# Strassen products in the first MLP of a two-layer decoder step, with the residual stream kept in DRAM

## The chip, the cores and the metric

The kernel runs on one core of one Trainium2 chip, in one launch. The metric is the device time of the launch in microseconds (us), the median of several executions. One more execution was taken with a hardware profile; its rows are the ones read below. A core has one matmul engine (TensorE, PE in the rows, its weight loads PEld), a vector engine (VectorE, DVE), a scalar engine (ScalarE, ACT), GpSimd (POOL), and queues that issue DMA transfers (SP's, ACT's and POOL's among them). Each engine takes its instructions strictly in the order in which they stand in its own list; a matmul result goes into PSUM banks and is read from there by DVE or ACT.

## The reference, cut to what matters

One step of a decoder with two layers runs on 512 prompt tokens and 8 sample tokens; the kernel treats them as one block of 520 columns. Layer 0 mixes tokens by causal pooling and then runs an MLP; after it, keys and values are projected once (`w_kv`), and layer 1 attends over them, projects, and runs its own MLP. What the change touches is the MLP:

```
def _rmsnorm(x, g):
    return x * lax.rsqrt(jnp.mean(x * x, axis=-1, keepdims=True) + RMS_EPS) * g

def _mlp_block(x, g, w_up, w_down):
    h = jnp.square(jax.nn.relu(_rmsnorm(x, g) @ w_up))   # 1024 -> 4096
    return x + h @ w_down                                # 4096 -> 1024
```

The samples also need 'summaries' of their cached pages (`_compress`: blocks of 32 cached rows times `cmp_w1`, then SiLU, then `cmp_w2`). They depend on the cache alone, so the kernel makes them beside the first MLP.

## The kernel before, in words

**Layout.** x stands transposed in SBUF, `xT`, as 8 tiles of 128 features by 520 tokens. Every large matmul is 128x128 weights against 260 columns, in a 32-bit format that keeps fewer mantissa bits. For full precision each operand is split in a rounded part and the rest (`whi`/`wlo`, `xh`/`xl`, `hh`/`hl`), and three products are summed: hi by hi, hi by rest, rest by hi. ACT rounds (L147, L181), DVE subtracts (L148, L182).

**Normalisation is deferred.** Since the MLP squares a ReLU, the kernel multiplies the unnormalised x by the gain alone, and scales the result by 1/mean(x^2) (`rstd2`) behind the down projection. The mean needs the squares of all 8 tiles: ACT squares, POOL adds six of them into `sqacc` (`add_square`, L224), PE sums over the partitions (`mean_tok`, L235), DVE reads the sums (L240, L242). `spread` (L245) makes the 128x520 `rstd2` from them: diagonal tiles on DVE (L250), two matmuls (L252, L253).

**Layer 0's MLP before** (`mlp`, L615) is the plain product. `split_x` (L260) makes xh and xl of each of the 8 tiles of x as soon as it is ready. `dense` (L151) makes 48 matmuls for each of 32 tiles of 128 hidden features, and as many for each of the 8 output tiles in each of 4 chunks of the down projection: 32x48 + 32x48 = 3072. It works in four PSUM banks under the tag `mm`. `yacc` (128x8x520) collects the output. Between tiles the loop takes a step of a filler, `compress_samples`, which gathers pages by POOL's indirect DMA (L361), permutes them (L372), transposes them on PE (L385), splits them (ACT L386, DVE L387) and multiplies them (L391) into two PSUM banks that stay taken until it ends. Those two are of the four banks under the tag `aux`.

**Layer 1's MLP before** (`fast_mlp`, L690) multiplies in quarters by Strassen's rule, in Winograd's form: for 256 hidden features the product of 2x2 blocks of weights with 2x2 blocks of x takes 7 products (`product`, L185) of 12 matmuls, 84 in place of 96. For that, `fast_w` (L313) makes three sums of weight blocks on DVE, and `fast_x` (L273) makes seven left-hand terms of x: for each j of 0 to 3 it scales tiles j and j+4 on ACT (L281), makes four sums and differences on DVE (L291, L292, L294, L297) and splits seven terms (ACT L286, DVE L287). The three terms `first` have tiles of their own, the four others take the place of xh and xl. The down projection is plain, in 8 chunks of 512 hidden features, 16 products of 12 matmuls in each, into the `aux` banks; its products stand between those of the next chunk's up projection.

**Order.** A scheduler sets each engine's list from the code's order and its own estimates; what it made of the start of the first MLP is shown below for both kernels.

## Time and profile before

| | us |
|---|---|
| median of 3 timed runs | 1197.63 (1195.52 to 1200.01) |
| the profiled execution | 1202.7 |
| its span in the trace | 1200.9 |
| PE busy in the span | 1156.1 (96%) |

Within the span the first MLP goes from about 50 us (the end of the pooling mixer's projection) to 452 us, keys and values follow, then attention, the output projection until 829 us, and layer 1's MLP from there to the end. The profile gives for each engine its busy time, the clock that the throttle granted TensorE in each stretch (1.00 is the level of 2.4 GHz, 0.5 that of 1.2 GHz), and for each wait what ended it. A row of a timeline is: start, duration, engine, line, operation, the tile written and the tiles read, and in square brackets the idle time ahead of it with what released it. Where instructions overlap in the engine's pipeline, the distance between two starts is the price of one, not the duration.

### The profile page before, as it was taken

Reading aid. Unit: us, or ns where it says so; the run is one execution under the profiler, and the core shown is the slowest. Engines: PE = TensorE matmul, PEld = TensorE weight load, DVE = VectorE, ACT = ScalarE, POOL = GpSimd, SP = SyncE. Lnnn points to the kernel's source line nnn. Section 1 sums busy time; section 2 is a strip of 40 time slices with the busy share of each in tenths; the row PEclk is TensorE's granted clock in tenths of the full one; section 3 lists DMA queues with packets and bytes.
Section 4 is the critical chain, followed back from the end, with each engine's and each line's share of the span. In section 5 each row is a group of like instructions: output and inputs, shape, how many; then the busy total and the mean of one; then the engine's idle time right before and its main releaser. Section 6 shows DMA issues by size and latency. Waiting matters only on the chain.

```text
span 1200.9 us, 22704 instructions
## 1 busy us (share of the span) xinstructions
PE 1156.1 (96%) x9163; PEld 1081.8 (90%) x9163; DVE 747.5 (62%) x1732; ACT 544.0 (45%) x1152; POOL 253.6 (21%) x287
## 2 busy tenths in 40 slices
PE   4999999999999999999899999979999999999996
PEld 4999999999999999999876566778999999999996
DVE  5844234444453574576588677648966686776885
ACT  4443233223323433453366565725764443544445
POOL 3500000000031020243358544631000000000032
PEclk9899999999999999999999999989999999999998
DMA  9454333324223236443411220261223323333201
GB/s 258 153 192 141 97 98 122 92 86 132 71 72 123 71 106 211 131 106 100 89 36 45 72 71 19 44 178 61 80 97 106 106 71 115 97 106 106 72 35 72
DMA packets 106511, 121.30 MB, mean 101 GB/s; under 512 B 5640, under 2 KB 93312, under 8 KB 106143
## 3 DMA queue, kind: packets, MB, share of 16 engines
q1 hardware_dynamic: 93159, 103.42, 28.0%
q0 software_dynamic: 4224, 12.17, 3.0%
q10 hardware_dynamic: 9024, 4.28, 1.3%
q8 instruction: 72, 1.18, 0.4%
q14 instruction: 32, 0.26, 0.1%
HBM read 111.50 MB, written 12.98 MB: 104 GB/s over the span
## 4 chain that ended last, share of the span: by engine, by line
PE 90%; DVE 4%; DMA 3%; ACT 1%; issue 1%; SPq 0%; DVEq 0%; ACTq 0%
PE mm L160 45%; PE mm L190 14%; PE aux L190 13%; PE mm L1151 3%; PE aux L1198 3%; PE aux L1225 3%; PE aux L391 2%; DMA wraw<-in_pool_w_dram 1%; DMA wraw<-in_w_up_dram 1%; DVE wlo L148 1%; PE aux L1023 1%; DMA spill<-xT 1%; PE aux L435 1%; PE mm L576 1%; PE aux L385 1%
## 5 line engine op out<-in xcount | busy, mean ns | idle before, releaser
L147 ACT ACTIVATE whi<-wraw 128x1024 fp32r<-128x1024 f32 (+1 forms) x95 | 99.9, 1055 | 302.3 <-PE mm L160 291.7
L160 PE MATMUL mm<-xh,whi 128*128 128x260 f32 (+1 forms) x976 | 208.5, 287 | 9.2 <-DVE xT L1298 5.8
L160 PE MATMUL mm<-xl,whi 128*128 128x260 f32 (+1 forms) x976 | 208.3, 287 | 0.8 <-issue 0.6
L160 PE MATMUL mm<-xh,wlo 128*128 128x260 f32 (+1 forms) x976 | 207.1, 286 | 0.4 <-issue 0.4
L148 DVE TENSOR_TENSOR wlo<-wraw,whi 128x1024 fp32r<-128x1024 f32 (+1 forms) x95 | 119.4, 1259 | 131.5 <-ACT whi L147 131.1
L160 PEld LDWEIGHTS mm<-xh,whi 128*128 128x128 f32 (+1 forms) x976 | 155.8, 190 | 11.9 <-DVE xT L1298 6.0
L160 PEld LDWEIGHTS mm<-xl,whi 128*128 128x128 f32 (+1 forms) x976 | 155.4, 190 | 1.9 <-issue 1.1
L160 PEld LDWEIGHTS mm<-xh,wlo 128*128 128x128 f32 (+1 forms) x976 | 155.1, 190 | 1.3 <-issue 1.0
L190 PE MATMUL aux<-hl,whi 128*128 128x260 f32 x448 | 125.2, 282 | 0.0
L190 PE MATMUL aux<-hh,whi 128*128 128x260 f32 x448 | 124.8, 282 | 0.0
L190 PE MATMUL aux<-hh,wlo 128*128 128x260 f32 x448 | 122.6, 283 | 0.0
L181 ACT ACTIVATE whi<-wraw 128x512 fp32r<-128x512 f32 x112 | 66.3, 626 | 106.6 <-PE mm L190 83.0
L160 PE MATMUL mm<-hh,whi 128*128 128x260 f32 x512 | 103.1, 283 | 0.0
L160 PE MATMUL mm<-hh,wlo 128*128 128x260 f32 x512 | 103.0, 283 | 0.0
L160 PE MATMUL mm<-hl,whi 128*128 128x260 f32 x512 | 103.0, 282 | 0.0
L182 DVE TENSOR_TENSOR wlo<-wraw,whi 128x512 fp32r<-128x512 f32 x112 | 75.5, 698 | 30.4 <-ACT whi L181 29.7
L1184 POOL TENSOR_SCALAR s<-s,psm,gate 128x128 f32<-128x128 f32 (+3 forms) x128 | 79.9, 637 | 41.3 <-DVE psm L1181 14.0
L190 PEld LDWEIGHTS aux<-hl,whi 128*128 128x128 f32 x448 | 84.3, 188 | 0.0
L190 PEld LDWEIGHTS aux<-hh,whi 128*128 128x128 f32 x448 | 84.1, 188 | 0.0
L190 PEld LDWEIGHTS aux<-hh,wlo 128*128 128x128 f32 x448 | 82.7, 188 | 0.0
L779 POOL TENSOR_TENSOR yacc<-yacc,xT 128x520 f32<-128x520 f32 x8 | 11.3, 1407 | 330.4 <-DVE yacc L778 327.0
L160 PEld LDWEIGHTS mm<-hh,whi 128*128 128x128 f32 x512 | 79.3, 188 | 0.7
(338 smaller groups left out, 2617.7 us busy)
## 6 DMA issues: line engine op xcount, KB each, us to landing
wraw<-in_w_up_dram SPq DMA_DIRECT2D x32, 1024.0 KB, 6.4
wraw<-in_w_down_dram SPq DMA_DIRECT2D x32, 1024.0 KB, 5.1
wraw<-in_w_kv_dram SPq DMA_DIRECT2D x6, 1024.0 KB, 4.9
w<-in_cmp_w_dram ACTq DMA_DIRECT2D x32, 128.0 KB, 5.0
wraw<-in_w_qg_dram SPq DMA_DIRECT2D x8, 512.0 KB, 8.3
wraw<-in_w_o_dram SPq DMA_DIRECT2D x16, 256.0 KB, 6.5
rw<-in_state_win_dram SPq DMA_DIRECT2D x8, 512.0 KB, 3.4
out_win_sample_dram<-in_state_win_dram SPq DMA_DIRECT2D x8, 510.0 KB
```

What stands on the lines that cost most here:

```text
L147: S.activation(h_, raw_ap, AF.Copy)
L148: (eng or V).tensor_tensor(l_, raw_ap, f(h_), OP.subtract)
L160: T.matmul(o[n][:m, :HN], w[:, kt, :m], x[:, n * HN : (n + 1) * HN], start=(i == 0 and pi == 0), stop=(i == len(kts) - 1 and pi == 2),)
L181: S.activation(hi, raw_ap, AF.Copy)
L182: V.tensor_tensor(lo, raw_ap, f(hi), OP.subtract)
L190: T.matmul(o, w_[:, kt], x_[kt][:, xs], start=(start and kt == 0 and pi == 0), stop=(kt == HK - 1 and pi == 2), skip_group_check=True,)
L385: T.transpose(b[:, h * P : (h + 1) * P], perm[:, kv * 4 + h].rearrange("p a d -> p (a d)"), ident)
L391: T.matmul(acc[kv], w_[:, kv, b2], o_[:, kv, b2 : b2 + 512], start=(t == 0 and i == 0 and b2 == 0), stop=(t == 7 and i == 2 and b2 == 1),)
L1151: T.matmul(b[:, : k1 - k0], qs[r][:, qt * P : (qt + 1) * P], ks[br][i][:, k0:k1], start=(i == 0), stop=(i == 1),)
L1184: G.tensor_scalar(st_[r], st_[r], sm[:, r : r + 1], gate[:, qt, c : c + 1], OP.mult, OP.mult)
L1198: T.matmul(o[par * HD : (par + 1) * HD], lhsT(par), pTs[par], start=start, stop=stop, skip_group_check=True,)
L1225: T.transpose(b[:, r * P : (r + 1) * P], sts[par][r][:, kt * P : (kt + 1) * P], ident)
```

## The change

There is now one `mlp`, Strassen's in the up projection, and both layers use it.

- Layer 0's x is no longer split by `split_x` but by `fast_x`, inside the MLP's own pool. In the code it stands behind `mean_tok` of the same x.
- `yacc` is gone. The down projection collects in `xT` itself. The old x is written to DRAM at the start of either MLP, by 8 DMAs on POOL's queue (L621), and read back tile by tile on ACT's queue in the chunk before the last (L709).
- Layer 0's down projection is the one of layer 1: products in halves, in the `aux` banks, between the up projection's products. The filler takes a step at every fifth product, and one at each of the 16 products of the last chunk.
- The filler's tiles are smaller: `perm`, `oh` and `ol` hold 512 columns for each of k and v in turn, `gat` has one buffer in place of two, `part` five in place of six.

```diff
-        x1 = split_x(gT[:, 16:24])
         sqacc = [st.tile([P, TOK], F32, name="sqacc")]
         for k in range(KT):
             add_square(st, sqacc, k)
...
+    def mlp(layer, xs, mean, mp, filler=None, finish=None):
+        xd = dram.tile([P, KT, TOK], F32, name=f"xd{layer}")
+        for k in range(KT):
+            nc.gpsimd.dma_start(xd[:, k], xT[k])
...
-        yacc = mp.tile([P, KT, TOK], F32, name="yacc")
+        steps = Steps(filler(mp) if filler else None, 8)
...
-                y = yacc[:, m]
+                y = xT[m]
...
-                    else:
+                    elif c < nc_ - 1:
                         V.tensor_tensor(y[:, hn], o, y[:, hn], OP.add)
                     if n and c == nc_ - 2:
+                        x = mp.tile([P, TOK], F32, name="xr", tag="sq", bufs=2)
+                        nc.scalar.dma_start(x, xd[:, m])
                         V.tensor_tensor(y, y, rstd2, OP.mult)
-                        G.tensor_tensor(y, y, xT[m], OP.add)
+                        G.tensor_tensor(y, y, x, OP.add)
+                    if c == nc_ - 1:
...
+                        V.tensor_tensor(t[:, hn], o, rstd2[:, hn], OP.mult)
+                        V.tensor_tensor(y[:, hn], y[:, hn], t[:, hn], OP.add)
+                        if n:
+                            add_square(mp, sqacc, m)
...
-                for s_ in "uuududdudududdd" if c else "uuuuuuu":
+                for q, s_ in enumerate("uuududdudududdd" if c else "uuuuuuu"):
                     next(u if s_ == "u" else d)
+                    if q % 5 == 4:
+                        steps()
...
-    mean1 = mlp(0, x1, mean0, compress_samples)
+    with pool("mlp0") as mp:
+        first = [[mp.tile([P, HK, HN], F32R, name=f"first{i}{j}") for j in range(2)] for i in range(3)]
+        x1 = fast_x(gT[:, 16:24], mp, first)
+        mean1 = mlp(0, x1, mean0, mp, compress_samples)
```

What the scheduler makes of it at the start of the first MLP is seen on three engines. On PE before, the first products of the MLP (L160 with `xh`, `xl`) stand right behind the pooling mixer's last ones (`dh`, `dl`):

```order
L160 MATMUL mm<-dl,whi 128x260
L160 MATMUL mm<-dh,wlo 128x260
L160 MATMUL mm<-xh,whi 128x260 [waits DVE_49,Activation_49]
L160 MATMUL mm<-xl,whi 128x260
L160 MATMUL mm<-xh,wlo 128x260
L160 MATMUL mm<-xh,whi 128x260 [waits Activation_49]
```

and after, the sums over partitions (L235), the first of which waits for POOL, stand between them:

```order
L160 MATMUL mm<-dl,whi 128x260
L160 MATMUL mm<-dh,wlo 128x260
L235 MATMUL aux<-ones,sqacc 128x1 [waits Pool_49]
L235 MATMUL aux<-ones,sqacc 128x1 x3
L235 MATMUL aux<-ones,sqacc 8x1
L235 MATMUL aux<-ones,sq 128x1 [waits Activation_49]
L235 MATMUL aux<-ones,sq 128x1 x3
L235 MATMUL aux<-ones,sq 8x1
L190 MATMUL mm<-first_483,whi 128x260 [waits DVE_49,Activation_49]
L190 MATMUL mm<-first_485,whi 128x260 [waits Activation_49]
L190 MATMUL mm<-xh,whi 128x260 [waits DVE_49,Activation_49]
L252 MATMUL aux<-dg,ones 128x512 [waits DVE_49]
```

So the mean of x has moved ahead of every product of the MLP on PE. On DVE before, the splits of x (L267) stand between the updates of xT (L590), and the reading of the mean (L240) behind them all:

```order
L590 SCALAR_TENSOR_TENSOR xT<-mm,gT,xT 128x260 [waits PE_49] x2
L148 TENSOR_TENSOR wlo<-wraw,whi 128x1024 [waits DMAHW2_49,Activation_49]
L590 SCALAR_TENSOR_TENSOR xT<-mm,gT,xT 128x260 [waits PE_49]
L267 SCALAR_TENSOR_TENSOR xl<-xT,gT,xh 128x520 [waits Activation_49]
L148 TENSOR_TENSOR wlo<-wraw,whi 128x1024 [waits Activation_49]
L267 SCALAR_TENSOR_TENSOR xl<-xT,gT,xh 128x520 [waits Activation_49] x2
L240 TENSOR_SCALAR ma<-aux 128x4 [waits PE_49]
```

and after, it stands ahead of the first sum of weights (L313) and of `fast_x`'s first part (L291):

```order
L592 SCALAR_TENSOR_TENSOR xT<-mm,gT,xT 128x260 [waits PE_49] x16
L240 TENSOR_SCALAR ma<-aux 128x4 [waits PE_49]
L242 TENSOR_SCALAR ma<-aux 8x1
L313 TENSOR_TENSOR wsum<-wraw 128x512 [waits DMASW6_49,Pool_49]
L624 RECIPROCAL ma<-ma 128x5 [waits DVE_49]
L291 TENSOR_TENSOR part<-relu 128x260 [waits DMASW2_49,DMASW7_49,DMASW1_49,DMAHW6_49,Activation_49,Pool_49]
L313 TENSOR_TENSOR wsum<-wsum,wraw 128x512 [waits DVE_49]
L313 TENSOR_TENSOR wsum<-wraw 128x512
L250 TENSOR_SCALAR dg<-ident,ma 128x128 [waits DMAHW1_49,DVE_49]
```

Everything that the Strassen products need of DVE now stands behind the mean. On POOL before, the six adds into `sqacc` stand alone:

```order
L602 DMA out_pool_sample_dram<-us 8x1024 [waits Pool_49]
L224 TENSOR_TENSOR sqacc<-sqacc,sq 128x520 [waits Activation_49]
L224 TENSOR_TENSOR sqacc<-sqacc,sq 128x520 [waits Activation_49,Pool_49] x5
L361 DMA gat<-in_cache_kv_pages_dram,idx 128x512 [waits DVE_49,PE_49]
```

and after, the eight writes of x (L621) stand between them:

```order
L603 DMA out_pool_sample_dram<-us 8x1024 [waits Pool_49]
L621 DMA xd_595<-xT 128x520 [waits DVE_49] x2
L224 TENSOR_TENSOR sqacc<-sqacc,sq 128x520 [waits Activation_49]
L621 DMA xd_595<-xT 128x520 [waits DVE_49]
L621 DMA xd_595<-xT 128x520 [waits DMASW3_49,DVE_49]
L224 TENSOR_TENSOR sqacc<-sqacc,sq 128x520 [waits Activation_49,Pool_49]
L621 DMA xd_595<-xT 128x520 [waits DMASW4_49,DVE_49]
L621 DMA xd_595<-xT 128x520 [waits DMASW5_49,DVE_49]
L224 TENSOR_TENSOR sqacc<-sqacc,sq 128x520 [waits Activation_49,Pool_49]
L621 DMA xd_595<-xT 128x520 [waits DMASW6_49,DVE_49]
L621 DMA xd_595<-xT 128x520 [waits DMASW7_49,DVE_49]
L224 TENSOR_TENSOR sqacc<-sqacc,sq 128x520 [waits Activation_49,Pool_49] x3
```

Five of the six adds now have DMA issues ahead of them or between them on POOL. From attention on, the lists are the same in both kernels but for `yacc` and the writes and reads of x.

## Rows read from the trace of the kernel before

**Rows 1.** The page: span, and busy time of each engine.
```profile
span 1200.9 us, 22704 instructions
...
PE 1156.1 (96%) x9163; PEld 1081.8 (90%) x9163; DVE 747.5 (62%) x1732; ACT 544.0 (45%) x1152; POOL 253.6 (21%) x287
```

**Rows 2.** Windows (us; busy us and count of PE, PEld, DVE, ACT, POOL; granted clock; DMA).
```profile
340.00:452.00 112.00, 112.00 (x926) 111.45 (x925) 59.87 (x84) 37.39 (x55) 23.04 (x15) 1.00 0.28 90
...
900.00:1000.00 100.00, 100.00 (x836) 100.00 (x835) 71.41 (x136) 43.60 (x87) 0.00 (x0) 1.00 0.34 106
```

**Rows 3.** Chain of waits from 30 us on: start, duration, what.
```profile
38.09 18.56 PE mm L160 x154
56.65 2.02 PE aux L235 x20
...
64.33 0.86 PE aux L252 x2
65.19 0.31 PE aux L253 x2
```

**Rows 4.** Windows around the start of the first MLP.
```profile
49.50:58.70 9.20, 9.20 (x81) 9.11 (x79) 7.47 (x8) 4.13 (x7) 8.27 (x6) 1.00 0.35 94
58.70:66.00 7.30, 7.30 (x41) 6.52 (x42) 5.22 (x15) 3.44 (x8) 2.39 (x3) 0.77 0.86 318
```

**Rows 5.** Timeline of POOL: a DMA issue, the six adds, and an add in layer 1.
```profile
31.32 0.55 POOL L602 DMA_DIRECT2D out_pool_sample_dram<-us  x1
...
43.52 11.03 POOL L224 TENSOR_TENSOR sqacc<-sqacc,sq 128x520 f32<-128x520 f32 x6 [11.64 <-ACT sq L222]
...
813.38 1.42 POOL L224 TENSOR_TENSOR sqacc<-sqacc,sq 128x520 f32<-128x520 f32 x1 [4.12 <-ACT sq L222]
```

**Rows 6.** Timeline of DVE at the start of the first MLP.
```profile
40.50 1.08 DVE L590 SCALAR_TENSOR_TENSOR xT<-mm,gT,xT 128x260 f32<-128x260 f32 x2 [0.22 <-PE mm L160]
...
58.70 0.16 DVE L240 TENSOR_SCALAR ma<-aux 128x4 f32<-128x4 f32 x1 [1.74 <-PE aux L235]
...
59.18 1.17 DVE L250 TENSOR_SCALAR dg<-ident,ma 128x128 f32<-128x128 f32 x5
...
63.99 0.69 DVE L372 COPY perm<-gat 128x1024 f32<-128x1024 f32 x1 [0.18 <-DMA gat<-in_cache_kv_pages_dram,idx]
```

**Rows 7.** Timeline of DVE at the start of layer 1's MLP.
```profile
834.12 0.41 DVE L294 TENSOR_TENSOR part<-relu,part 128x260 f32<-128x260 f32 x1
834.46 0.41 DVE L297 TENSOR_TENSOR part<-relu 128x260 f32<-128x260 f32 x1
...
847.20 0.69 DVE L182 TENSOR_TENSOR wlo<-wraw,whi 128x512 fp32r<-128x512 f32 x1
847.80 0.69 DVE L182 TENSOR_TENSOR wlo<-wsum,whi 128x512 fp32r<-128x512 f32 x1
```

**Rows 8.** Window of the start of layer 1's MLP.
```profile
829.00:845.50 16.50, 13.31 (x85) 11.48 (x84) 15.38 (x49) 14.70 (x36) 0.00 (x0) 0.90 0.20 64
```

**Rows 9.** Timeline of PE there.
```profile
828.89 1.07 PE L235 MATMUL aux<-ones,sqacc 128*128 128x1 f32 x10
...
836.88 1.33 PE L252 MATMUL aux<-dg,ones 128*128 128x512 f32 x2 [2.13 <-DVE dg L250]
...
840.13 0.42 PE L190 MATMUL mm<-first,wlo 128*128 128x260 f32 x1
840.34 0.42 PE L190 MATMUL mm<-first,whi 128*128 128x260 f32 x1
```

**Rows 10.** Groups by shape, DVE, 870 to 1147 us: busy, mean ns, idle before.
```profile
L776 DVE TENSOR_TENSOR yacc<-aux,yacc 128x260 f32<-128x260 f32 x89 | 37.9, 426 | 22.6 <-PE aux L190 22.5
```

**Rows 11.** Window of attention.
```profile
612.00:780.00 168.00, 163.82 (x1148) 106.73 (x1148) 125.57 (x591) 109.55 (x325) 103.71 (x154) 1.00 0.17 48
```

**Rows 12.** Chain of waits at the end of the first MLP.
```profile
371.65 80.53 PE mm L160 x671
...
452.21 0.49 DVE relu L664 x2
```

More of the change, by code (lines that the diff above doesn't have):

```diff
@@ L303, in part @@
     def part(tp):
[L304 removed]
+        return tp.tile([P, 264], F32, name="part", tag="part", bufs=5)[:, :HN]
     def fast_w(raw, tp):
@@ L367, in compress_samples @@
         for t in range(8):
+            w1, gat = loaded.pop(t)
+            perms = []
+            for kv in range(2):
+                perm = tp.tile([P, 4, 2, HD], F32, name="perm", tag="perm", bufs=2)
+                V.tensor_copy(perm, gat.rearrange("p a (k h d) -> p k h a d", k=2, h=4)[:, kv])
+                perms.append(perm)
             if t < 7:
                 load(t + 1)
-            w1, gat = loaded.pop(t)
-            perm = tp.tile([P, 8, 2, HD], F32, name="perm", tag="perm", bufs=1)
-            V.tensor_copy(perm, gat.rearrange("p a (h d) -> p h a d", h=8))
-            oh = tp.tile([P, 2, 513], F32R, name="oh", tag="oh", bufs=1)
-            ol = tp.tile([P, 2, 513], F32R, name="ol", tag="ol", bufs=1)
-            for o_ in (oh, ol):
-                S.activation(o_[:, :, 512:513], ones[:, :2].unsqueeze(2), AF.Copy, scale=0.0)
             wh = tp.tile([P, 2, 2, P], F32R, name="w1h", tag="w1h", bufs=1)
@@ L382, in compress_samples @@
             for kv in range(2):
+                oh, ol = [tp.tile([P, 513], F32R, name=n, tag=n, bufs=1) for n in ("oh", "ol")]
+                for o_ in (oh, ol):
+                    S.activation(o_[:, 512:513], ones[:, :1], AF.Copy, scale=0.0)
                 b = bank()
                 for h in range(4):
[L385 to L387 removed]
+                    T.transpose(b[:, h * P : (h + 1) * P], perms[kv][:, h].rearrange("p a d -> p (a d)"), ident)
+                S.activation(oh[:, :512], b, AF.Copy)
+                V.tensor_tensor(ol[:, :512], b, f(oh[:, :512]), OP.subtract)
                 yield
@@ L395, in compress_samples @@
                 yield
-        out = tp.tile([P, 2, 512], F32, name="sums", tag="perm", bufs=1)
+        out = tp.tile([P, 2, 512], F32, name="sums", tag="gat", bufs=1)
         for kv in range(2):
@@ L786, in fast_mlp @@
                 u = up(c, i)
-                for s_ in "uuududdudududdd" if c else "uuuuuuu":
+                for q, s_ in enumerate("uuududdudududdd" if c else "uuuuuuu"):
                     next(u if s_ == "u" else d)
+                    if q % 5 == 4:
+                        steps()
         S.activation(const.tile([P, 1], F32, name="warm", tag="warm", bufs=2), f(hs[nc_ - 1][3][0][:, 0:1]), AF.Sqrt)
-        finish(mp, wd[nc_ - 1], hs[nc_ - 1], yacc, rstd2, sqacc[:1])
+        sqacc = [mp.tile([P, TOK], F32, name="sqacc", tag="hh", bufs=8)]
+        if finish:
+            finish(mp, wd[nc_ - 1], hs[nc_ - 1], rstd2, sqacc)
+        else:
+            for _ in down(nc_ - 1):
+                steps()
+            mean2 = mean_tok(sqacc)
+            steps.rest()
+            return mean2
     for b_ in range(NB):
```

88 lines of the change are left out of this document (8 added, 80 removed).

## The prediction

> **What bounds the kernel now.** I read the page first: PE is busy for 1156.1 of 1200.9 us [rows 1], so only fewer matmuls or fewer gaps on PE can shorten the time. Then the windows of the first MLP, which show whether PE there waits for anything: in the 112 us from 340 to 452 it is busy throughout at a granted clock of 1.00, while DVE is busy for 59.87 and ACT for 37.39 [rows 2]. The first MLP is bound by the number of its matmuls. Layer 1, which already works by Strassen's rule, is bound by PE too: from 900 to 1000 us it is 100% busy, with DVE at 71 [rows 2]. The same rule should therefore hold PE full in layer 0 as well, once it runs. Last I read the chain of waits and the windows around the start: in the kernel before PE goes from the mixer's projection into the MLP with no gap. Of the 9.20 us from 49.50 to 58.70 none is idle; in the 7.30 us behind it the granted clock is 0.77, which costs 0.23 x 7.3 = 1.7 us [rows 4]. So the start costs 1.7 us today. That is the place to look at, since the order shows the change rebuilding it.
>
> **Fewer matmuls.** Strassen's 84 per 256 hidden features in place of 96 make 16 x 12 = 192 fewer (2880 in place of 3072). A matmul of this shape takes 100 us / 836 = 0.1196 us [rows 2]. The gain is 192 x 0.1196 = **-23.0 us**, all of it on the path, as PE is full there.
>
> **The start.** In the kernel before, `split_x` prepares x tile by tile, and PE follows. In the changed one three things stand in a row before PE can work, and I add them up.
>
> First, POOL. The mixer's projection is 96 matmuls from 38.09 on, at 18.56/154 = 0.1205 us, so PE is through at 49.6 [rows 3]. The mean needs the six adds on POOL. They take 11.03 us in the kernel before, or 1.84 each, beside a busy DVE; one in layer 1 takes 1.42 [rows 5]. I take three of each, 9.8 us. The first can begin when the second tile of x is updated, at 41.6 at the latest [rows 6], and squared, which I put at 42.4. From there six of the eight DMA issues still stand among them: 6 x 0.55 = 3.3 [rows 5], and I take 3.6, as a write of a whole tile is the larger transfer. POOL ends at 42.4 + 9.8 + 3.6 = 55.8 (54 to 57.5 with all adds at either price). Before, it ended at 54.55 and held up nobody.
>
> Second, the mean: 20 small matmuls of `mean_tok` take 2.02 us [rows 3], up to twice that if PE's clock has fallen by then. DVE reads the result at about 58.5 (57.5 to 60). That is when L240 ran before, too (58.70, [rows 6]); but then 33 products of the MLP had been done, and now none has, because DVE cannot pass L240: all 44 operations that `fast_x` has on DVE are queued behind it, and ACT's roundings wait for them in turn.
>
> Third, DVE's train behind L240. Until the last of the seven terms of x is split, the order has these on DVE: 45 operations of 128x260 at 0.34 (the distance of two starts in layer 1, 834.12 and 834.46), 14 of 128x512 at 0.60 (847.20 and 847.80) [rows 7], five for the diagonal, 1.17, and two halves of the permutation, 0.69 [rows 6], and some 0.5 of small ones. Sum: 15.3 + 8.4 + 1.2 + 0.7 + 0.5 = 26.1 us. So PE is free to run on at 58.5 + 26.1 = 84.6. Meanwhile only those products can run whose terms are ready; the order has 62 of them ahead of the first that needs the last terms: 62 x 0.12 = 7.4 us of PE's work, and with the mean (2.0) and `spread` (0.86 + 0.31 [rows 3]) 10.6. Of the 35.0 us from 49.6 to 84.6, 24.4 are lost; 1.7 were lost before. The term is **+22.7 us**. Its bounds: if the adds cost 1.42 each, the clock holds and DVE needs 24, +18.5; if the adds cost 1.84, the mean 4 and DVE waits for ACT's roundings for 2 us, +28.
>
> **The clock behind the start.** PE is then mostly idle for 35 us. In layer 1's start, behind a wait of 2.13 us, products follow each other at 840.13 and 840.34, that is 0.21 apart and not 0.12 [rows 9], the lower of the two levels, and the window's mean is 0.90 [rows 8]. Behind a longer idle stretch I expect the lower level at least as long. Bounds: nothing, if the sparse products bring the clock up by themselves, and 5 us; I take **+2 us**, near to what 0.10 of 16.5 us makes (1.7).
>
> **The down projection and its banks.** The products of the down projection now go into `aux`, of which the filler keeps two from the third chunk on. Two are left for them, where the plain MLP had four `mm` banks. While an up product stands between two of the down products this costs nothing: DVE's eviction takes 0.43 us [rows 10], against 1.43 us of a product of 12. Where down products follow one another, at the end of the last chunk, DVE has two more operations and a square for each tile, and the slack that I count from the order falls under 1.5 us. **+2.5 us**, between 0 and 6.
>
> **What lies beside.** The 16 writes of x and 16 reads move 4 x 2.1 MB. In the middle of the MLP DMA is busy for 0.28 to 0.34 of the time [rows 2]; only at the start do they meet the loads of weights, which have 25 us more time than before. The reads are issued from ACT a chunk ahead. If that cover failed, PE would wait 2 us for each of a few tiles. The smaller tiles of the filler make as many operations on DVE and ACT as before (each half the size), and steps at every fifth product are in time for the end of the last chunk. Layer 1 changes by its writes of x alone, which stand beside PE's work. I take nothing for all of these.
>
> **Sum.** -23.0 + 22.7 + 2 + 2.5 = +4.2 us. The profiled execution should go from 1202.7 to 1206.9 us; it stands 0.4% above the median of the timed runs, so the median from 1197.63 to **1201.8 us**. A measurement of this kernel can tell about 0.5%, 6 us, from no change. The forecast is no change that can be told: the whole gain goes into the start.
>
> **Rivals.**
>
> *B, the two banks (slower).* Where the loop makes two down products in a row ("dd"), 24 times from the third chunk on, the second needs the bank whose eviction stands on DVE behind two splits of weights and a sum (2 x 0.60 + 0.6 us). If that queue and the eviction (0.43) together come to more than the 1.43 us of one product, PE waits about 0.5 to 0.8 us each time. Price: 24 x 0.5 = 12 us, time 1213.8 (up to 1221). For it: DVE is busy for 71 of 100 us in layer 1 [rows 10 and 2], and the filler adds to that. Against it: layer 1 with four banks shows 22.5 us in which DVE waits for PE ahead of these evictions, not the other way round [rows 10].
>
> *C, the start costs as much as layer 1's (faster).* There the same `fast_x` begins before the last tile is ready: in the 16.5 us from 829 to 845.5 [rows 8], PE does 60 products (7.2 us), the mean (2 x 1.07) and `spread` (1.2), and loses 6. If the start here cost only that, the term would be 6 - 1.7 = +4.3 in place of 22.7 and 2, and the time 1197.6 - 23.0 + 4.3 + 2.5 = 1181.4. For it: the operations are the same. Against it: in layer 1 many splits and two whole products stand on DVE and PE ahead of the mean, and in the order of the changed kernel nothing of `fast_x` does.
>
> *D, the clock (slower).* If the many short waits of the down projection in two banks drew the clock down each time, the product behind each of the 24 places would run at the lower level: 24 x 12 x (0.21 - 0.12) = 26 us on top of B's 12, time about 1240. Against it: attention has 4.2 us of waits scattered over 168 us, at a granted clock of 1.00 [rows 11]. The Trainium skill speaks for it: its page "TensorE: Matmul & The Clock Gate", section "A second HAM failure mode: psum-queue depth-cycling", says that short idle spells between groups of matmuls that cycle through PSUM banks can make the clock swing between its two levels. The trace does not agree so far, so the chance is small.
>
> That the change doesn't do what it says is excluded by the order: the 192 matmuls are gone.
>
> **How the numbers follow.** A, the forecast, 0.67, with 1195 to 1209; B 0.17, C 0.13, D 0.03. The range that leaves out no more than 2 in 10 covers A with its bounds and the lower half of B: 1190 to 1215. Faster by over 0.5% (under 1191.6): C, and a tail of A, 0.14. Slower by over 0.5% (over 1203.6): B, D, and a third of A, 0.42. Within: 0.44.
>
> **What would show it right or wrong.** Right: between 50 and 85 us PE is mostly idle; the reading of the mean comes at 57.5 to 60 us with all of `fast_x` behind it; PE runs without gaps from about 85 us at the latest, first at a low clock; the last product of the down projection, at 452.2 us before [rows 12], ends at 455 to 458; all later stages take as long as before. Wrong: if PE is full from 65 or 70 us on (C, the train is shorter than I count or more products run in it), if it shows waits of half a microsecond for `aux` banks from the third chunk on (B), or if the granted clock of the stretch from 90 to 440 us is under 1.00 (D). If the sum of the start is right and the total still differs, the mis-sized term is the clock or the end of the last chunk.

## The result: 1211.9 us, slower by 1.2%

| | before | after |
|---|---|---|
| median of the timed runs, us | 1197.04 (1195.52 to 1200.01) | 1211.9 (1208.98 to 1217.26) |
| ratio, with its 95% interval | 1 | 1.0116 [1.0086, 1.0146] |
| span of the profiled execution, us | 1200.9 | 1215.5 |
| from the mixer's last product to the block of 51 `w_kv` products, us | 423.1 | 438.9 |
| from there to the end, us | 728.1 | 728.6 |

The prediction was 1201.8, range 1190 to 1215. The time is in the range, but 10 us above the number, and "within 0.5%" was wrong: it is slower. The last two lines of the table say where to look: all of it lies ahead of the block of `w_kv` products, which stands in the chain of both kernels as 6.11 us of 51 products (at 472.77 us before, at 486.90 after).

The page of the changed kernel has 192 matmuls fewer (9163 in [rows 1]), and more of DVE's and ACT's time in it.

```profile
span 1215.5 us, 22977 instructions
...
PE 1148.4 (94%) x8971; PEld 1068.2 (88%) x8971; DVE 874.1 (72%) x2064; ACT 607.1 (50%) x1340; POOL 261.0 (21%) x303
```

The start, in windows (columns as in [rows 2]). In [rows 4] no time of the first 9.20 us was idle; now PE waits in each of the three windows up to 75 us, its clock falls to 0.50, and from 95 to 420 us it is full at 1.00.

```profile
49.50:58.70 9.20, 4.43 (x21) 4.04 (x21) 1.26 (x6) 3.36 (x6) 5.81 (x5) 0.69 0.37 111
58.70:66.00 7.30, 5.53 (x14) 3.37 (x14) 7.30 (x21) 6.67 (x18) 0.70 (x1) 0.50 0.42 118
66.00:75.00 9.00, 4.66 (x13) 3.23 (x13) 9.00 (x23) 3.41 (x10) 8.70 (x2) 0.50 0.62 233
...
95.00:420.00 325.00, 325.00 (x2642) 321.48 (x2641) 241.60 (x443) 157.53 (x336) 20.87 (x17) 1.00 0.37 118
```

What PE waits for between 36 and 500 us, as far as it is over 1 us (who waits, for what: us in total, times, the longest). Three are at the start (for `first`, `sqacc` and `wsum`), two of 1.7 and 1.4 us in the MLP's last chunk. The first and largest is none of these: it stands behind the MLP, where keys and values begin.

```profile
PE aux L813 <- DVE kvt L786: 8.4, 1, 8.4
PE mm L190 <- ACT first L286: 6.3, 4, 3.1
PE aux L235 <- POOL sqacc L224: 5.5, 1, 5.5
PE aux L393 <- DVE ol L389: 1.7, 1, 1.7
PE aux L190 <- DVE xT L706: 1.4, 1, 1.4
PE mm L190 <- DVE wsum L313: 1.4, 1, 1.4
```

The kernel before has one row in the same stretch, the same wait:

```profile
PE aux L860 <- DVE kvt L833: 1.6, 1, 1.6
```

I follow this wait back. DVE's timeline: it waits 10.57 us at L148, a split of the `w_kv` weights; the copy of the key norm (L255) and the scaling of the first keys (L786) stand behind it in DVE's list, though what they need has been there since 472 us.

```profile
466.00 1.02 DVE L250 TENSOR_SCALAR dg<-ident,r 128x128 f32<-128x128 f32 x5
477.59 1.23 DVE L148 TENSOR_TENSOR wlo<-wraw,whi 128x1024 fp32r<-128x1024 f32 x1 [10.57 <-ACT whi L147]
478.73 0.16 DVE L255 COPY rstd<-aux 128x8 f32<-128x8 f32 x1
...
479.94 1.43 DVE L786 TENSOR_TENSOR kvt<-mm,rstd 128x260 f32<-128x260 f32 x4
```

The split needs ACT's rounding (L147), which starts at 476.50. What these two work on has long been there: it is the third load of `w_kv`, issued at 429.51, whose last part landed at 434.52. ACT is held up by its own list. Ahead of the rounding stand four DMA issues (L347, `w`, weights for summaries), which hold it from 464.73 to 476.40. By the semaphores' times in the trace the third of them goes out at 470.97, when the `spill` has landed (470.89), and the fourth at 476.02, when the fifth load of `w_kv` has (476.00): each waits for the semaphore on which that transfer was counted. In ACT's timeline:

```profile
464.73 11.67 ACTq L347 DMA_DIRECT2D w<-in_cmp_w_dram  x4
476.50 2.01 ACT L147 ACTIVATE whi<-wraw 128x1024 fp32r<-128x1024 f32 x2 [11.57 <-DMA sampb<-in_sampb_dram]
```

The second row names `sampb`, which is counted on the same semaphore as the third load; its own last part landed at 476.70, after the start of the rounding. In the kernel before it is the same: the fifth load has landed at 465.76, the fourth issue follows at 465.78, the rounding of the third load at 466.26.

In SP's queue the fifth load is issued behind the `spill` (L851), which writes all of xT to DRAM, 2080 KB, and can be issued only when the last tile of xT is finished:

```profile
449.12 0.37 SPq L133 DMA_DIRECT2D wraw<-in_w_kv_dram  x1
461.86 0.34 SPq L851 DMA_DIRECT2D spill<-xT  x1
463.63 0.37 SPq L133 DMA_DIRECT2D wraw<-in_w_kv_dram  x1
```

The windows there: DMA is busy until 475 us, first with the spill and then with the load, PE runs dry, and comes back at half its clock.

```profile
465.00:470.00 5.00, 5.00 (x44) 5.00 (x44) 1.85 (x11) 0.00 (x0) 0.00 (x0) 1.00 0.93 293
470.00:475.00 5.00, 2.00 (x10) 1.02 (x8) 0.00 (x0) 0.00 (x0) 0.00 (x0) 1.00 1.08 344
475.00:480.00 5.00, 0.00 (x0) 0.00 (x0) 2.41 (x4) 2.49 (x3) 0.55 (x1) 0.63 0.14 41
480.00:485.00 5.00, 4.58 (x21) 4.59 (x22) 2.89 (x9) 2.62 (x4) 0.01 (x1) 0.50 0.80 263
```

Before, the order is the same, behind a last product at 452.2 [rows 12], and PE still had work of its own to cover all but 1.6 us:

```profile
453.68 0.34 SPq L898 DMA_DIRECT2D spill<-xT  x1
454.81 0.37 SPq L133 DMA_DIRECT2D wraw<-in_w_kv_dram  x1
```

**The account.** To compare kernels I cut the stretch into windows of 5 us and add up PE's idle time, and its busy time times (1 - granted clock). "Start" is the first 40 us behind the mixer, "behind" the rest of the chunks, "tail" the last chunk, "seam" what lies between the MLP and the block of 51 products. All in us, from one profiled execution of each; a first number is idle time, a second low clock. The start, which e1 and e4 leave as it is, comes out at 23.9, 23.9 and 24.2 in after, e1 and e4.

| kernel | stretch | start | behind | tail | seam | ratio to before |
|---|---|---|---|---|---|---|
| before | 423.1 | 0 + 1.7 | 0 | 0 | 1.6 + 0 | 1 |
| after | 438.9 | 14.7 + 9.2 | 0 | 3.5 | 8.4 + 3.0 | 1.0116 |
| e1 | 429.4 | 14.7 + 9.2 | 0 | 3.5 | 1.7 + 0 | 1.0061 |
| e2 | 421.2 | 0 + 1.7 | 0 | 0 | 0 | 0.9976 |
| e3 | 438.0 | 15.7 + 7.3 | 0 | 3.5 | 7.2 + 4.1 | 1.0098 |
| e4 | 433.8 | 14.7 + 9.5 | 0 | 0.2 | 7.9 + 1.9 | 1.0094 |
| e5 | 437.5 | 14.2 + 6.4 | 0 + 1.7 | 3.5 | 6.2 + 4.6 | 1.0165 |
| e6 | 439.8 | 17.7 + 6.4 | 0.2 + 1.6 | 3.5 | 8.4 + 2.0 | 1.0159 |
| e7 | 426.5 | 17.1 + 7.5 | 0.2 + 0 | 0.2 | 1.4 + 0 | 1.0035 |
| e8 | 433.0 | 11.4 + 6.7 | 0 | 3.5 | 8.5 + 1.8 | 1.0110 |
| e9 | 428.8 | 13.4 + 5.1 | 4.1 + 2.5 | 0.2 | 1.3 + 0 | 1.0027 |
| e10 | 429.3 | 16.9 + 2.0 | 3.8 + 3.0 | 0.3 | 1.3 + 0 | 1.0019 |
| e11 | 422.6 | 14.4 + 4.0 | 0 + 1.7 | 0.3 | 1.3 + 0 | 0.9973 |
| e12 | 418.4 | 9.5 + 3.5 | 0.9 + 0.9 | 0.2 | 1.3 + 0 | 0.9945 |

From the block to the end the profiled executions of these kernels take between 723.3 and 734.6 us, though little was changed there (with e1's edit the spill runs beside this stretch, and e4's banks hold for layer 1's last chunk as well). The stretch is therefore the surer measure of an edit, and the ratio that of the kernel.

### The profile page after: what moved, and what is told of

It is laid out like the page before. It is cut to its first block, busy times and chain, and to the rows that moved or that the text cites. A ratio compares the mean times of both kernels' runs of the same rounds, so it can differ in the third digit from the quotient of the medians.

```text
span 1215.5 us, 22977 instructions
## 1 busy us (share of the span) xinstructions
PE 1148.4 (94%) x8971; PEld 1068.2 (88%) x8971; DVE 874.1 (72%) x2064; ACT 607.1 (50%) x1340; POOL 261.0 (21%) x303
## 4 chain that ended last, share of the span: by engine, by line
PE 84%; DVE 7%; DMA 3%; issue 2%; POOL 2%; ACT 2%; SPq 0%; ACTq 0%; DVEq 0%; POOLq 0%
PE mm L190 27%; PE aux L190 27%; PE mm L160 14%; PE aux L1151 3%; PE aux L1178 3%; PE mm L1104 3%; PE aux L393 2%; DMA xt<-in_x_prompt_dram 1%; DVE wlo L182 1%; DVE s L1109 1%; PE aux L235 1%; DMA sampb<-in_sampb_dram 1%; DMA wraw<-in_w_up_dram 1%; PE aux L813 0%; POOL sqacc L224 0%
## 5 line engine op out<-in xcount | busy, mean ns | idle before, releaser
L190 PE MATMUL aux<-hh,whi 128*128 128x260 f32 x960 | 269.0, 282 | 1.8 <-DVE xT L706 1.4
L190 PE MATMUL aux<-hl,whi 128*128 128x260 f32 x960 | 270.0, 283 | 0.0
L190 PE MATMUL aux<-hh,wlo 128*128 128x260 f32 x960 | 266.1, 283 | 0.0
L190 PE MATMUL mm<-first,whi 128*128 128x260 f32 x768 | 152.9, 291 | 9.6 <-ACT first L286 7.5
L190 PE MATMUL mm<-xh,whi 128*128 128x260 f32 x512 | 145.5, 284 | 0.0
L190 PE MATMUL mm<-xl,whi 128*128 128x260 f32 x512 | 145.1, 284 | 0.3 <-DVE xl L287 0.3
L190 PE MATMUL mm<-xh,wlo 128*128 128x260 f32 x512 | 144.7, 284 | 0.0
L190 PEld LDWEIGHTS mm<-first,whi 128*128 128x128 f32 x768 | 123.3, 192 | 13.6 <-ACT first L286 10.6
L160 PE MATMUL mm<-xh,whi 128*128 128x260 f32 (+1 forms) x464 | 104.3, 292 | 6.9 <-DVE xT L1251 5.2
L190 PE MATMUL mm<-first,wlo 128*128 128x260 f32 x384 | 110.4, 288 | 0.4 <-DVE wlo L182 0.4
L160 PE MATMUL mm<-xl,whi 128*128 128x260 f32 (+1 forms) x464 | 104.4, 290 | 0.2 <-DVE xl L1194 0.2
L160 PE MATMUL mm<-xh,wlo 128*128 128x260 f32 (+1 forms) x464 | 103.6, 290 | 0.0
```

The lines of the kernel that those rows point to most:

```text
L160: T.matmul(o[n][:m, :HN], w[:, kt, :m], x[:, n * HN : (n + 1) * HN], start=(i == 0 and pi == 0), stop=(i == len(kts) - 1 and pi == 2),)
L190: T.matmul(o, w_[:, kt], x_[kt][:, xs], start=(start and kt == 0 and pi == 0), stop=(kt == HK - 1 and pi == 2), skip_group_check=True,)
```

## The experiments

### The seam behind the MLP: e1 and e2

Theory: the spill ahead of the fifth load costs the 10 us that the prediction missed. Rival: they lie in the start, which would be dearer than it looks. In e1 the spill's DMA is issued behind the last load of `w_kv` in SP's queue, and nothing else is changed; e2 is the same edit in the kernel before.

```diff
-                nc.sync.dma_start(spill, xTt)
+                with tc.issue_after(kvload):
+                    nc.sync.dma_start(spill, xTt)
```

> The changed kernel with one edit: the 2 MB write of x to DRAM for the later layers (spill) is queued on SP behind the last load of the key/value weights, not ahead of the last two. Seam theory: in the changed kernel PE waits 8.4 us behind the first MLP, because the fifth weight load stands behind that write and DVE's and ACT's work for it blocks the evictions; and it runs 2.7 us slower behind the wait. Then the time falls from 1211.9 to about 1204 (1202 to 1207), and the first transposes of keys come about 8 us sooner. Rival, the excess over the forecast lies within the MLP (two banks, the start): unchanged, within 3 us of 1211.9.

> The kernel before with the same edit. Seam theory: PE waited only 1.6 us there, since it still had products of keys and values to do when the MLP ended; so it gains 0 to 3 us (1194 to 1198). Rival, the write costs whatever kernel it stands in: 6 us or more gained.

e1: 1.0061 [1.0041, 1.0080], 6.6 us less than the changed kernel by the ratios. In its SP queue the fourth and the fifth load (447.93 and 462.42) follow each other, the sixth and last is issued at 472.18, and the spill at 472.65:

```profile
447.93 14.87 SPq L134 DMA_DIRECT2D wraw<-in_w_kv_dram  x2
...
472.65 0.63 SPq L855 DMA_DIRECT2D spill<-xT  x1
```

and PE's wait is what it was in the kernel before:

```profile
PE aux L816 <- DVE kvt L788: 1.7, 1, 1.7
```

The seam's 11.4 us in the account are 1.7, the start's are what they were. e2: 0.9976 [0.9958, 0.9993]; the edit is worth 2.9 us there, as the wait of 1.6 us goes. The seam theory holds: the spill's place is the cause. The gain in time is 6.6 us where the trace's stretch shows 9.5. The fifth load now lands at 468.12, and ACT's fourth issue of `w` follows at 468.14, so it is through ACT's list that the spill reached PE, and not through weights that the split lacked. Whether moving the issues of `w` out of ACT's list would do as much, with the spill where it was, was not run.

### The last chunk: e4

Theory: in the last chunk down products follow each other and two `aux` banks are too few; they may use the four `mm` banks, which no up product needs any more.

```diff
-                    o = bank()[:, :HN]
+                    o = bank("mm" if c == nc_ - 1 else "aux")[:, :HN]
```

> The changed kernel with one edit: the 16 down products of the first MLP's last chunk go into the four mm banks and not into the two that the filler leaves in aux. Two-bank theory: the waits of PE there (1.4 us for an eviction, 1.7 for the filler's split) shrink, 1 to 3 us gained. Rival, DVE is what limits this stretch: within 1 us, and the last update of x still comes some 3 us behind the last product.

Measured 1.0094 [1.0069, 1.0118]. The two waits of 1.7 and 1.4 us are gone, with 0.2 left, the tail's loss goes from 3.5 to 0.2; the time falls by some 2.6 us by the ratios, with intervals that overlap. What the trace shows is near the predicted size of this term (2.5 us). A new wait has come up in its place, in the seam of the account: the first `w_kv` products need an `mm` bank that DVE still empties, here and in e7 and e9 to e12.

```profile
PE mm L160 <- DVE relu L715: 1.3, 1, 1.3
```

### The start: e3, e5, e6, e8

Theory: the start's 24 us come from the mean standing ahead of everything. The order of the changed kernel shows why the scheduler put it there: `sq`, `sqacc` and `rstd2` shared memory with tiles of the stage before, which the MLP's pool reuses. e3 gives them a pool of their own:

```diff
+    m0_ = ExitStack()
+    m0 = m0_.enter_context(pool("m0"))
...
-        sqacc = [st.tile([P, TOK], F32, name="sqacc")]
+        sqacc = [m0.tile([P, TOK], F32, name="sqacc", tag="acc")]
...
-        rstd2 = mp.tile([P, TOK], F32, name="rstd2")
+        rstd2 = mq.tile([P, TOK], F32, name="rstd2", tag="acc" if m0 else "rstd2")
```

> The changed kernel with one edit: the tiles of the squares and of their sum stand in memory that the MLP's pool does not reuse, so that the splitting of x need not wait for the mean. Start theory: DVE's train of about 26 us then begins when x is ready (48.6 us) and not when the mean is read (57.4), so PE is full from about 75 us in place of 83.7: 8.5 us gained (6 to 10), 1203.5. Rival, the train is not what PE waits for (weights, POOL or the clock are): less than 3 us gained. Second rival, it comes back at the seam, where a load sets the time: less than 3 us gained in all, with the MLP ending 8 us sooner.

Measured 1.0098 [1.0071, 1.0125], 2 us less where 8.5 (6 to 10) were expected; the start still loses 23.0. In e3 many splits of x do stand ahead of the mean. But POOL's timeline shows that its last add takes 9.13 us beside them, where the first took 1.32:

```profile
37.05 1.32 POOL L224 TENSOR_TENSOR sqacc<-sqacc,sq 128x520 f32<-128x520 f32 x1
...
54.84 9.13 POOL L224 TENSOR_TENSOR sqacc<-sqacc,sq 128x520 f32<-128x520 f32 x1 [3.67 <-ACT sq L222]
```

So the mean comes at 67.96 in place of 57.44, and DVE and PE stop for it there (PE 6.5 us for that add). The add ends at 63.97, 1.15 us behind the last operation of DVE's train:

```profile
62.14 0.68 DVE L313 TENSOR_TENSOR wsum<-wraw 128x512 f32<-128x512 f32 x1
67.96 0.16 DVE L240 TENSOR_SCALAR ma<-aux 128x4 f32<-128x4 f32 x1 [5.14 <-PE aux L235]
```

What the other tiles gained, the add took back.

e5 goes on from e3: the reading of the mean and `spread` are held until the last product of the first chunk.

```diff
+            if m0 and c == 0:
+                last = next(i for i in reversed(nc.cur_bb.bb.instructions) if "Matmult" in type(i).__name__ or "Matmul" in type(i).__name__)
+                with tc.issue_after(last):
+                    rstd2 = scale()
```

> The changed kernel with the mean's tiles in memory of their own, as in e3, and with the mean, its reading and the making of rstd2 put behind the first chunk of the up projection on PE. In e3 the start was only some 3 us shorter than in the changed kernel: DVE stopped at the reading of the mean for 5.14 us, since one of POOL's adds took 9.13 us beside DVE's train, where it takes 1.32 alone. Theory: DVE's train, not the mean itself, is what the start needs, and POOL starves beside it; with the mean out of the way PE is full about 24 us behind the mixer's end in place of 35.6, and the time is 11 us (8 to 13) under the changed kernel's, near 1.003 of before. POOL's adds take several us each and hold up nobody. Rival, the train is slowed by something else (the permutation that waits for POOL's gathers, the weights): 3 us gained or less, as in e3.

Measured 1.0165 [1.0140, 1.0190]: above the changed kernel's 1.0116, where 11 us less were expected. No wait for the mean is left in e5, and the start loses 20.6 + 1.7 in place of 23.9, no more. Of its timeline of DVE, the first two rows stand beside POOL's adds, where an operation of 0.42 us takes up to 2.46; and POOL's last add takes 10.84 beside DVE's train:

```profile
48.04 2.46 DVE L287 TENSOR_TENSOR first<-part,first 128x260 fp32r<-128x260 f32 x1
50.42 1.85 DVE L287 TENSOR_TENSOR xl<-relu,xh 128x260 fp32r<-128x260 f32 x2
52.19 0.42 DVE L294 TENSOR_TENSOR part<-relu,part 128x260 f32<-128x260 f32 x1
```

```profile
55.31 10.84 POOL L224 TENSOR_TENSOR sqacc<-sqacc,sq 128x520 f32<-128x520 f32 x1 [3.67 <-ACT sq L222]
```

The theory that the mean's place is what costs the start does not hold. What PE waits for in e5 is ACT's terms of x (`first`, 6.7 us), DVE's splits of weights (`wlo`, 3.0) and DVE's terms (`first`, 1.9): the train on DVE and ACT sets the time. Its last split ends at 74.09, 29.3 us behind the mixer's end, in place of 35.5:

```profile
73.67 0.42 DVE L287 TENSOR_TENSOR xl<-part,xh 128x260 fp32r<-128x260 f32 x1
```

Of the 6.2 us gained, the matmuls of the mean and of `spread` take some 3.2 us [rows 3]: they had lain in PE's idle time, and now stand where PE is full. That e5 is some 6 us slower as a whole the stretch does not show (437.5 against 438.9); its time behind the block is 734.0 us, and why stays open.

e6 adds to e5 that the mixer finishes the tiles in the order in which `fast_x` takes them (0, 1, 4 and 5 first), and that more of the MLP's tiles do not wait for memory of the stage before.

```diff
-        for gi in range(4):
+        for gi in (0, 2, 1, 3):
...
-        x1 = fast_x(gT[:, 16:24], mp, first)
+        x1 = fast_x(gT[:, 16:24], m0, first)
```

> e5, and the temporary tiles of the splitting (relu, part) in memory of their own, and the mixer's groups in the order 0, 2, 1, 3, so that the tiles of x that are split in pairs (j and j+4) are ready early. Theory: part of DVE's train moves to the time before the mixer's end; the start is 5 to 7 us shorter again, 16 to 18 us under the changed kernel, near 0.998 of before. Rival, the pieces wait for the tiles first, or ACT is the next bound: within 2 us of e5.

Measured 1.0159 [1.0131, 1.0186]; the start loses 24.1 us. An earlier begin of the train is no earlier end: its first part starts 7.5 us ahead of the mixer's end, in e5 1.0 behind it, and its last split ends 30.9 us behind it, in e5 29.3. DVE's operations of 0.68 us take up to 2.74 beside POOL's adds, and DVE waits 2.15 us for ACT's `xh`.

e8 is e3 with the last two adds on DVE instead of POOL, to test the price of the slow add by itself.

```diff
-                G.tensor_tensor(sqacc[0], sqacc[0], t, OP.add)
+                (V if k in dve else G).tensor_tensor(sqacc[0], sqacc[0], t, OP.add)
```

> e3 with the last two of the six adds of squares on DVE in place of POOL. Theory (POOL starves beside DVE's train): the wait of DVE at the reading of the mean (5.14 us in e3) falls under 2 us and PE is full 3 to 4 us sooner than in e3; the time is 3 to 4 us under e3's. Rival (the mean is late because the squares or PE are): no change against e3, the wait stays.

Measured 1.0110 [1.0085, 1.0136]. PE's wait for the adds is 0.2 us in place of 6.5, the start loses 18.1 in place of 23.0, and the stretch is 5.0 us shorter than e3's; the time does not show it within its interval (0.0012 above e3). The slow add is real and worth some 5 us of the stretch; a gain in time is not shown.

### Both sure edits together: e7

e7 is e6 with the edits of e1 and e4.

> e6 with the edits of e1 (the write of x behind the key/value weights) and of e4 (last chunk in the mm banks). Theory: the three costs add, as they stand in different places of the time: 17 + 6.6 + 2 us under the changed kernel, near 0.990 of before (0.987 to 0.994). Rival, with the start gone the seam is set by DVE's tail, and e1's gain does not add: 0.995 or more.

Measured 1.0035 [1.0011, 1.0060]. Against e6 the stretch falls by 13.3 us, the seam's 9.0 and the tail's 3.3 among them, and the time by 1.2%. The two edits add up, the start's edits give nothing; the 0.990 that was expected fails with the start.

### A start that needs less of DVE: e9 to e12

New theory: the train is too long for what PE can do beside it. Three of the seven terms of x, t2, t3 and t4, are needed by Strassen's products alone. In e9 the first two groups of 256 hidden features are multiplied in plain quarters, which need b11, t1 = b12 - b11, b21 and b22 alone; the three other terms are made while PE works on them. Each such group costs 12 more matmuls (1.4 us). The mean and `spread` are now made behind the second chunk; all else is as in e7.

```diff
+            for m in range(2):
+                product(o[m], w1[m], xs["b11"])
...
+            for m in range(2):
+                product(d[m], w1[m], xs["t1"])
...
+            for m in range(2):
+                product(o[m], w2[m], xs["b21"], start=False)
...
+            for m in range(2):
+                product(d[m], w2[m], xs["b22"], start=False)
+                V.tensor_tensor(rs[m][:, t2], d[m], cs[m], OP.add)
```

> e7, with the first chunk of the up projection (two groups of 256 hidden features) as plain products of quarters, 8 per group in place of 7, which need only four of the seven terms of x and no sums of weights; the other three terms are made meanwhile. e5 to e7 moved the mean and the tiles and left the start's loss on PE (idle time and lower clock) at 20 to 25 us, as in the changed kernel (23.9). Theory: the loss is DVE's train against the 62 products that can run beside it; here PE has 192 products, and needs about 10 us of DVE before the first of them can run through. The loss falls to under 12 us; 24 products more cost 2.9 us; the time is 8 to 12 us under e7's, near 0.995 of before (0.992 to 0.998). Rival: the start is bound by something else that is late then (weights from DRAM, ACT, POOL): loss still 18 us or more, time as e7 or slower.

Measured 1.0027 [1.0011, 1.0043], no better than e7. PE waits once for 9.3 us, for ACT's copy of a product. My reading, which e12 tests: the copy needs a `part` tile, and all five are taken by temporaries of the three other terms.

```profile
PE mm L192 <- ACT part L723: 9.3, 1, 9.3
```

e10 also makes the squares for the mean later, behind the first plain group:

```diff
+                    lastact = next(i for i in reversed(nc.cur_bb.bb.instructions) if "Activation" in str(i.engine))
+                    with tc.issue_after(lastact):
+                        for k in range(KT):
+                            add_square(m0, mean, k)
```

> e9, and the squares of x on ACT, and with them the adds on POOL, put behind the splitting of x, so that neither stands beside DVE's first pieces. Theory: DVE's operations that took 1.3 to 2.5 us beside POOL's adds in e5 (0.42 alone) run at their own speed, and ACT's roundings come sooner: the start loses 2 to 4 us less than in e9. Rival: POOL's adds meet the DVE work of the second group in the same way and PE waits there: no gain.

Measured 1.0019 [0.9997, 1.0041]. The low clock at the start shrinks from 5.1 to 2.0, but the wait of 9.3 us is there again, and another has grown: in DVE's list a copy of the samples' filler waits 7.16 us for its gather, with the splits of x behind it, and PE waits 8.3 us for one of these.

```profile
PE mm L192 <- DVE first L291: 9.5, 2, 8.3
...
60.85 0.76 DVE L382 COPY perm<-gat 128x512 f32<-128x512 f32 x2 [7.16 <-DMA gat<-in_cache_kv_pages_dram,idx]
```

e11 is e10 with one plain group in place of two.

```diff
-                early = more is not None and c == 0 and i < 2
+                early = more is not None and c == 0 and i < 1
```

> e10 with only the first of the two groups of the first chunk as plain products. 12 products fewer, 1.4 us; but the second group needs the other three terms about 14 us after the mixer's end, and DVE has some 19 us of work until then. Theory (DVE's train): PE waits 3 to 6 us there, so 2 to 4 us slower than e10. Rival: DVE is ahead by then, 1.4 us faster than e10.

Measured 0.9973 [0.9957, 0.9989], faster than both kernels, and level with e2 (0.9976). The direction is the rival's, the size is neither's: 5.5 us under e10 by the ratios. In e11 that copy waits only 0.18 us for its gather, though the wait for ACT's copy (9.5 us) stays; that this is the difference was not tested by itself.

e12 goes back to two groups and takes both waits away: the copies of products get two tiles of their own, and the filler's first steps are held back to the place in the code where they stand, behind what DVE and ACT have to do there.

```diff
-                t = part(mq)
+                t = part(mp, 2 if m0 else 5)
...
-                        steps()
+                        with ExitStack() as st_:
+                            if more and c <= 2:
+                                tr = nc.cur_bb.bb.instructions
+                                for e in ("Activation", "DVE"):
+                                    st_.enter_context(tc.issue_after(next(i for i in reversed(tr) if str(i.engine).endswith(e))))
+                            steps()
```

> Kernel: as e10_plain_squares_later (the first two groups of the first MLP in plain quarters, the other three terms of x made beside them, the squares behind them, the last chunk's banks and the spill as in e7_all), with two waits taken away that its trace showed: the copies of products have two tiles of their own in the MLP's pool, so that they no longer wait for the temporaries of x's terms (9.3 us at L720 there), and the samples' compression is held back to the second and third chunk, so that VectorE's queue has no copy in it that waits for a gather (7.2 us at L382 there). Theory: these two waits are what is left of the start in e10; without them the start loses under 10 us in all in place of some 20, PE passes from the plain groups into the fast ones without a gap over 2 us, and the kernel takes 8 to 14 us less than e10's 1199.94: 1186 to 1192, ratio to before 0.988 to 0.994. Rival: the terms of x are late on VectorE anyway (they end some 35 us behind the mixer whatever the tiles), so that PE waits for first or xl as long as it waited for the tile before, and the time stays at 1196 to 1200 (ratio 0.997 to 1.002).

Measured 0.9945 [0.9924, 0.9966], some 9 us under e10 by the ratios (8 to 14 expected). Both waits are gone. The longest that PE has left at the start is 5.0 us (none over 2 was expected), for a bank that DVE empties late:

```profile
PE mm L192 <- DVE relu L735: 5.0, 1, 5.0
```

and the windows show it working beside the making of the terms, at full clock from 55 us to 70:

```profile
50.00:55.00 5.00, 5.00 (x31) 4.88 (x31) 4.29 (x12) 4.62 (x11) 3.52 (x2) 0.72 0.98 329
55.00:60.00 5.00, 5.00 (x44) 5.00 (x43) 2.76 (x5) 2.59 (x7) 0.00 (x0) 1.00 0.19 76
60.00:65.00 5.00, 5.00 (x44) 5.00 (x43) 3.53 (x7) 3.87 (x10) 0.00 (x0) 1.00 0.02 3
65.00:70.00 5.00, 5.00 (x44) 5.00 (x44) 4.58 (x10) 3.92 (x9) 0.00 (x0) 1.00 0.00 0
70.00:75.00 5.00, 3.85 (x30) 3.44 (x29) 4.22 (x11) 2.36 (x6) 0.00 (x0) 1.00 0.00 0
75.00:80.00 5.00, 1.34 (x8) 1.03 (x8) 4.66 (x13) 4.12 (x9) 0.00 (x0) 0.67 0.87 314
```

The start loses 13.0 us in place of e10's 18.9, and 1.8 behind it in place of 6.8 (under 10 in all was expected, 14.8 it is). The two waits, taken away together, account for 10.9 us of e10's loss; what each is worth by itself is not shown. e12 is faster than the kernel before by 0.3 to 0.8%. Against e2, the kernel before with its spill later, the intervals overlap by 0.0008 (e2's begins at 0.9958): that Strassen's rule pays against that kernel is likely, not shown.

## Why the prediction was right and wrong

**The number: 1201.8 for 1211.9, and the range held it by luck.** The forecast A had 1195 to 1209; the measured time lies above all of it. The range went on to 1215 for the lower half of B, and B did not happen. What filled its place is a cost that the prediction had put at nothing (below).

**The start: right, nearly row by row.** POOL was to end at 55.8; it ended at 53.44, as its adds took some 1.3 us each, less than either price of [rows 5]. POOL's timeline has the last three, beside a DVE that waited:

```profile
49.42 4.02 POOL L224 TENSOR_TENSOR sqacc<-sqacc,sq 128x520 f32<-128x520 f32 x3
```

DVE was to read the mean at 58.5; it did at 57.44. The train behind it was to take 26.1; its last split of x stands at 83.11 in DVE's timeline, 25.7 later:

```profile
57.44 0.16 DVE L240 TENSOR_SCALAR ma<-aux 128x4 f32<-128x4 f32 x1 [8.88 <-PE aux L235]
...
83.11 0.42 DVE L287 TENSOR_TENSOR xl<-part,xh 128x260 fp32r<-128x260 f32 x1
```

PE was to be free to run on at 84.6; in PE's timeline the products are without a gap over 0.4 us from here to 420 us:

```profile
83.65 0.51 PE L190 MATMUL mm<-first,whi 128*128 128x260 f32 x2 [0.36 <-ACT whi L181]
```

Start and clock together were put at 22.7 + 2 = 24.7; the account gives 23.9 - 1.7 = 22.2. The split between them was off: the low clock is inside those 35 us, not behind them (9.2 of the 23.9 us), and PE's idle time is that much smaller; from 85 us on, where a low clock was expected, it is 1.00. So the sum describes this kernel; it does not follow that the mean's place is the cause of the whole of it, since e5 took the mean out and lost 22.3. One reading was wrong, without weight in the sum: when L240 ran in the kernel before, 58 products of the MLP had been done (154 - 96, [rows 3]), not 33.

**The rivals: as weighed.** C (a start like layer 1's) and B (waits of half a microsecond from the third chunk on) are both refuted by the window from 95 to 420 us, 325.00 of 325 us busy, and by the start's windows. D falls with the same row: the short waits that it starts from are not there, and the granted clock is 1.00. The page "TensorE: Matmul & The Clock Gate" of the Trainium skill, section "A second HAM failure mode: psum-queue depth-cycling", which spoke for D, has the clock swing where the engine idles between groups of matmuls; this stretch has no such idle time, so it neither bears the section out nor speaks against it.

**Matmuls: nearly.** The 192 are gone [rows 1, and the page above]. PE's full-clock work in the stretch (its length less the losses of the account) fell by 419.8 - 400.1 = 19.7 us, where 23.0 stood in the sum; the 3.3 between them I could not assign to a row. This term is what the account leaves over, so that the deviations below add up by themselves.

**The tail: right.** 2.5 was taken, 3.5 is in the account, and e4 takes 3.3 of it away (and brings 1.3 behind it). The last product of the down projection ended at 458.35, just past the 455 to 458 that were given.

**The step that failed: "What lies beside", and with it "all later stages take as long as before".** I put what stands behind the MLP at nothing. It cost (8.4 + 3.0) - 1.6 = 9.8 us, which is the miss: the other deviations (start -2.5, tail +1.0, matmuls +3.3) come to 1.8, and 4.2 + 9.8 + 1.8 = 15.8 is the difference of the stretches. The order was the same in both kernels, a spill of 2080 KB ahead of a load for whose landing ACT's list waits, with DVE and at last PE behind ACT, and the wait of 1.6 us in the trace of before said that the cover there was already used up. The prediction did not read that stretch: it followed the chain to the MLP's end at 452 us [rows 12], and priced the change's own transfers, not those that stand in line behind its last result. e1 shows it: this edit alone takes the wait from 8.4 to 1.7, the low clock with it, and 6.6 us from the time.

The wait grows by 6.8 us, and the times of the two traces split it, counted from the MLP's last product (458.35; before 452.18). The fifth load has landed 4.1 us later, 17.65 us behind that product in place of 13.58. Of this, 2.0 us are the spill's issue, 3.5 us behind the product in place of 1.5, as the last tile's update now has more operations behind it; for the other 2.1, a longer way from the spill's issue to the load's landing, I have no reason. PE's work that covers the load ends 1.6 us sooner, 13.65 us behind the product in place of 15.24: 12 of the 96 `w_kv` products ahead of the wait now stand in the MLP's tail. And from the load's landing to PE's first transpose of keys (L813, L860 before) it takes 1.1 us longer, 4.42 in place of 3.28, with two splits ahead of it on DVE in place of one.

From the block of 51 products on, the later stages did take as long as before: 728.6 and 728.1 us.

## What to carry to other kernels

A change that moves the end of a stage has to be followed past that end: look, in the trace of before, at every wait in the first 30 us behind it, and at each queue in which something large stands that needs the stage's last result; a small wait there is a cover that has run out. Look also at the DMA issues in the list of an engine that computes: one that waits for another transfer's landing holds up work whose operands have long been there. A stretch in which PE idles is worth only what the longest train in it takes: moving one thing (the mean) out of it gave little as long as the other train was nearly as long, and cost what the idle time had hidden; asking less of the train, with plain groups that need four of seven terms, gave in e11 and e12, and nothing in e9 and e10, where other waits took its place. And each edit of that kind brought up the next wait in line (a product's copy, a gather at the head of a queue, a bank), so its trace is to be read for the new first wait before it is judged.

## What the runs showed of the hardware

POOL and DVE hold each other up to a degree that I had not expected. An add of 128x520 on POOL takes 1.34 us with DVE idle (4.02 for three), and 9.13 (e3) and 10.84 (e5) beside a train of DVE operations nearly all of which read two tiles of SBUF; DVE's operations of 0.42 us take up to 2.46 beside POOL's adds. The Trainium skill says in "SBUF — State Buffer", section "Who interferes with whom", that such a DVE operation and a GpSimd one that reads SBUF exclude each other, by a lock held for the whole instruction. The trace agrees in kind, and shows who loses: against operations that follow each other without a gap POOL's add does not come through at all. It ends 1.15 us behind the last of them in e3 (63.97 and 62.82) and 1.15 behind the first pause in e5 (66.15 and 65.00), which is little less than the whole add alone.
